# One layer of a hybrid streaming encoder on one core: GpSimd in order of emission, small copies moved to VectorE, rests and stores of the delta-rule jobs placed anew

## The chip, the cores and the metric

The program runs on one core of one Trainium2 chip. A core has a matrix engine (TensorE, in the profile PE for the products and PEld for loading their stationary operand), a vector engine (VectorE, DVE), a scalar engine (ScalarE, ACT), a general engine (GpSimd, POOL) and SyncE (SP), which in this program issues the transfers between HBM and the on-chip memories. Each engine works through a list of its own, in order, and stops at an instruction whose inputs or whose destination are not ready.

The metric is the device time of one execution, in microseconds. The kernel before takes 2979.81 us, the median of three runs from 2978.62 to 2980.59.

## The reference

One encoder layer takes 512 prompt frames and 64 sample frames of width 2048, all in float32. What it computes, shortened:

```
mod = silu(c) @ w_ada + b_ada                       # six vectors of shift, scale and gate
h   = rmsnorm(x, norm1) * (1 + sc1) + sh1
a_q, a_k, a_v, a_r, a_lr, b_q, b_k, b_v, b_g, b_beta, b_alpha = split(h @ w_in)
# group A: gated linear attention, 4 heads
o_a, s_gla = recurrence(gla_step, st_gla, a_q, a_k, a_v, log_a)
# group B: gated delta rule, 8 heads of 128
q, k, v = silu(causal_dwconv([b_q, b_k, b_v], st_conv, gdn_conv_w))    # width 4
q, k = l2norm(q) * 128**-0.5, l2norm(k)
# per block: S_t = a_t (I - b_t k_t k_t^T) S_{t-1} + b_t k_t v_t^T,  o_t = S_t^T q_t,
#   with a solve by the unit lower triangle (I + strict_lower(beta k k^T * decay))
o_b, s_gdn = recurrence(gdn_step, st_gdn, q, k, v, g, beta)
o   = rmsnorm_per_head([o_a, o_b]) * gain * silu(gates)
x   = x + g1 * (o @ w_out)
h   = rmsnorm(x, norm2) * (1 + sc2) + sh2
x   = x + g2 * conv_ffn(h)                         # w_up, causal conv of width 3, w_down
y   = rmsnorm(x, final_norm)
```

Beside y, the last states of both recurrences and the last columns ahead of both convolutions are outputs, for the prompt and for the sample.

## The kernel before

**Stages.** Up to about 205 us the program transposes x, works out the modulation and the first columns of the input projection. From 205 to 880 us it computes the input projection of the delta-rule group head by head, with the recurrences of the heads beside it; from 880 to 1280 us the other group and the output projection; from 1280 us on the feed-forward part. Weights are float32, split into a high part (ACT, L599) and the remainder (DVE, L600) from a raw tile that SP loads (L598), and each product is made of three.

**How other work is put beside the projections.** One column tile of the projection is 16 steps of 6 matmuls. After each step `tick` advances the jobs: Python generators, the first of which may do one step of its work. `yield` ends the step, `yield WAIT` lets the next job in the list have it, and `rest(n)` is n times WAIT, so n steps of the projection (about 6 matmuls each) pass before the job emits more. A second generator, `ada_block`, works out the vectors of modulation that are wanted later: it loads weights into `xr` (L764), sums products with a scalar on DVE (L770, L772), and adds over the partitions by matmuls with one column (L778).

**What sets the order.** The Tile framework takes the operations as emitted, finds the dependences, and orders each engine's list by priority and by its own model of costs. The operations of a job on DVE and ACT go through `_Sooner` (all have line L1623), which gives them a priority of 80 places ahead; GpSimd's don't. So the lists of two engines need not be in the order of emission.

**One head of the delta rule.** The tiles q, k, v and g of the projection pass the convolution `gdn_conv` (q, k, v): ACT and DVE empty the two halves of the PSUM tile into `cb`, four small GpSimd copies (L916 to L919) put the columns in front of each half and save the last three columns, and ACT and DVE sum four shifted products. `put_s` sends the sample's columns to HBM (L900). Then the job `gdn`:

- it loads the head's decays (L173), and ACT makes two exponential tiles of them, which GpSimd masks (L181, L182);
- it normalizes q and k: sums of squares, L137 on DVE (adds epsilon), L138 on GpSimd (power of -1/2);
- it forms the strict lower triangle a, and `inverse16` inverts its 16x16 diagonal blocks. The blocks go to HBM (L340) and come back with one block to a lane (four loads, L345). After `rest(REST_D)` GpSimd does the substitution, 30 instructions of which each needs the one ahead (L347 to L354); below this is "the chain". Its result goes to HBM (L355), comes back spread over the partitions (two loads, L358), and DVE expands it (two L362);
- three levels double the size of the inverses by matmuls (the first at L238), and the states are carried from block to block (matmuls L276 to L305, states on DVE);
- the head's output is normalized: squares and sums, L137, L138, a scaling on ACT, four transposes (L144), a product with the gate on DVE, and a store by SP.

`gdn_heads` emits the tiles q and k of head h+1 ahead of v and g of head h, so the job of head h+1 begins while that of head h is in its recurrence: the chain of head h+1 and the norm of head h lie close together.

**Names that recur.** `bank` is a PSUM tile of the pool that all jobs share; `m`, `qkv`, `s`, `st`, `sq` are tiles of SBUF; `wh`, `wl` and `raw` are parts and raw tiles of weights; `xr` and `acc` belong to `ada_block`; `cm` is what L358 loads.

```
REST_D, REST_X, REST_T, REST_N, REST_G = 8, 16, 2, 2, 3
```

Here REST_D stands between the lane loads and the chain, REST_X behind the expansion, REST_T behind the norm of q and k, REST_N ahead of the transposes of the output, and REST_G in the other group.

Of the kernel before, what the change touches and what calls it, by code (L numbers as in the profile page):

```python
# [8 lines left out]
F32 = mybir.dt.float32  # L9
# [3 lines left out]
ALU = mybir.AluOpType  # L13
# [3 lines left out]
P = 128  # L17
# [17 lines left out]
REST_D, REST_X, REST_T, REST_N, REST_G = 8, 16, 2, 2, 3  # L35
# [60 lines left out]
class Kern:  # L96
    def __init__(self, tc, ctx, i, o):
# [4 lines left out]
        self.c = {}  # L102
        self.jv, self.ja = _Sooner(tc, tc.nc.vector), _Sooner(tc, tc.nc.scalar)

# [23 lines left out]
    def small(self, w):  # L128
        return self.sp.tile([P, w], F32, tag=f"s{w}", name=self.name(f"s{w}"))
# [5 lines left out]
    def rsqrt(self, out, src, n, parts=P):  # L135

        self.nc.vector.tensor_scalar_add(out[:parts, :n], src[:parts, :n], EPS)  # L137
        self.nc.gpsimd.tensor_tensor(out[:parts, :n], out[:parts, :n], self.mhalf[:parts, :n], op=ALU.pow)  # L138
# [16 lines left out]
    def gdn(self, qF, kF, x, gain, hcols, gb_src, s0, s_out, o_put, last_level):  # L155
# [25 lines left out]
        nc.gpsimd.affine_select(du, du, pattern=[[0, 4], [1, P]], compare_op=ALU.is_ge, fill=0.0, base=0, channel_multiplier=-1)  # L181
        nc.gpsimd.affine_select(dl, dl, pattern=[[0, 4], [-1, P]], compare_op=ALU.is_gt, fill=0.0, base=0, channel_multiplier=1)  # L182
        if pair:
            nc.gpsimd.memset(du[0:64, :, 64:P], 0.0)
# [4 lines left out]
        junk = self.half()  # L189
# [122 lines left out]
        junk = self.half()  # L312
# [10 lines left out]
        V.tensor_tensor(kF, kF, x["gate"](), op=ALU.mult)  # L323
        o_put(kF)
# [6 lines left out]
    def inverse16(self, a):  # L331
# [4 lines left out]
        nc, c, G = self.nc, self.c, self.nc.gpsimd  # L336
        pitch = 4 * P
        d0 = self.dp.tile([8 * (16 * pitch + 16)], F32, tag="d0", bufs=2, name=self.name("d0"))
        d1 = self.dp.tile([2, 32, 256], F32, tag="d1", bufs=2, name=self.name("d1"))
        nc.sync.dma_start(d0[:P * pitch].rearrange("(p f) -> p f", p=P), a.rearrange("p b t -> p (b t)"))  # L340
        lane = self.m()[:32].rearrange("p (w f) -> p w f", w=2)
# [12 lines left out]
        G.tensor_copy(xt, xx.rearrange("p i j -> p j i"))  # L354
        nc.sync.dma_start(d1.rearrange("w q f -> q w f"), lane)  # L355
        cm = self.sp.tile([P, 2, 4, 16], F32, tag="cm", bufs=1, name=self.name("cm"))
        for w in range(2):
            nc.sync.dma_start(cm[:, w], d1[w].rearrange("(b n) (i j) -> (n i) b j", b=4, i=16))  # L358
        sh = [P, 4, 8, 16]
        t, u = self.m4(), self.m4()  # L360
# [3 lines left out]
        yield from self.rest(REST_X)  # L364
        return u, t

    def gla(self, nb, qF, kF, g, x, s0, s_out, o_put):
# [103 lines left out]
        for f in range(2):  # L471
# [4 lines left out]
            o_put(f, dst)  # L476
# [419 lines left out]
    def put_s(self, name, col, write):  # L896
# [3 lines left out]
        self.nc.sync.dma_start(self.sd[name][:, col * TS:(col + 1) * TS], t)  # L900
# [7 lines left out]
    def gdn_conv(self, ps, t, dst, name, h):  # L908
# [3 lines left out]
        cb = self.ap.tile([P, 582], F32, tag="cb", bufs=1, name=self.name("cb"))  # L912
# [772 lines left out]
```

## Time and profile before

| | us |
|---|---|
| median of three runs | 2979.81 (2978.62 to 2980.59) |
| the profiled execution, its own time | 2981.26 |
| span of the profiled execution | 2979.5 |
| PE busy | 2863.4 (96%), 21060 instructions |
| DVE busy | 2050.0 (69%), 3234 |
| ACT busy | 1179.3 (40%), 2015 |
| POOL busy | 338.0 (11%), 609 |
| mean granted clock of TensorE | 0.98 |

A line of a group gives the source line, the engine, the operation, its output and inputs with partitions by elements and the count; behind the bar stand the busy time and the mean in ns, and the idle time of the engine just before, with what ended it. A line of the timeline begins with start and duration in us, and a bracket at its end gives the wait just before it and what released it (a name after `<-`). A line with a stretch `A:B` gives the stretch's length and then each engine's busy time with its number of instructions, the granted clock of TensorE as a share of full speed, and the load of the transfers. SPq is SP's own list of transfers.

### The profile page before, as it was taken

How to read it: one execution, taken by the hardware profiler on the slowest of the kernel's cores; microseconds unless marked ns; L12 is line 12 of the kernel's file. 1: busy time of each engine (PE TensorE's matmuls, PEld its weight loads, DVE VectorE, ACT ScalarE, POOL GpSimd, SP SyncE). 2: the span in 40 equal slices, each digit the busy share in tenths (PEclk: the TensorE clock that was granted, in tenths of full speed). 3: DMA queues.
4: the chain of work that ended last, by engine and by line, in shares of the span. 5: the costliest groups of instructions: out<-in, count | busy, mean ns of one | idle time of the engine just before them, and what ended most of it. 6: DMA issues, size and time to landing. Idle time of an engine off the chain costs nothing.

```text
span 2979.5 us, 52341 instructions
## 1 busy us (share of the span) xinstructions
PE 2863.4 (96%) x21060; PEld 2772.9 (93%) x21060; DVE 2050.0 (69%) x3234; ACT 1179.3 (40%) x2015; POOL 338.0 (11%) x609
## 2 busy tenths in 40 slices
PE   6998899999899999999999999999999999999998
PEld 3688888999889998999999999999999999999997
DVE  2366766667668867557888888888888865555555
ACT  4234444444445333245444444444444421222223
POOL 0004323333120000000011111111111100000000
PEclk8999999999999999999999999999999999999999
DMA  8864544444454446643333333333333473333221
GB/s 269 285 185 121 150 143 124 128 129 144 134 159 130 137 132 194 199 140 97 106 105 111 109 103 107 111 102 105 115 105 105 133 236 101 111 101 113 84 85 66
DMA packets 535446, 395.55 MB, mean 133 GB/s; under 512 B 59657, under 2 KB 465412, under 8 KB 535204
## 3 DMA queue, kind: packets, MB, share of 16 engines
q1 hardware_dynamic: 535204, 392.21, 44.0%
q8 instruction: 166, 2.72, 0.4%
q14 instruction: 76, 0.62, 0.1%
HBM read 356.47 MB, written 35.67 MB: 132 GB/s over the span
## 4 chain that ended last, share of the span: by engine, by line
PE 71%; DVE 3%; DMA 2%; POOL 1%; issue 1%; ACT 1%; SPq 0%; ACTq 0%; DVEq 0%; POOLq 0%
PE g L512 22%; PE bank L1301 11%; PE bank L1300 11%; PE bank L1302 11%; PE g L514 11%; DVE acc L772 1%; PE bank L405 1%; PE bank L144 1%; DMA xr<-in_w_ada_dram 1%; DMA xr<-in_x_prompt_dram 1%; PE bank L778 1%; DVE wl L600 0%; POOL m L352 0%; POOL m L351 0%; POOL s L138 0%
## 5 line engine op out<-in xcount | busy, mean ns | idle before, releaser
L1301 PE MATMUL bank<-slot,wh 128*128 128x290 f32 x2464 | 736.3, 299 | 0.0
L1300 PE MATMUL bank<-slot,wh 128*128 128x290 f32 x2464 | 734.0, 298 | 0.0
L1302 PE MATMUL bank<-slot,wl 128*128 128x290 f32 x2464 | 728.2, 296 | 0.0
L512 PE MATMUL g<-slot,wh 128*128 128x288 f32 x3168 | 551.7, 295 | 0.3 <-DVE slot L1070 0.3
L512 PE MATMUL g<-hh,wh 128*128 128x288 f32 x2048 | 473.1, 310 | 0.0
L1302 PEld LDWEIGHTS bank<-slot,wl 128*128 128x128 f32 x2464 | 470.8, 191 | 0.0
L1301 PEld LDWEIGHTS bank<-slot,wh 128*128 128x128 f32 x2464 | 469.8, 191 | 0.1
L512 PEld LDWEIGHTS g<-slot,wh 128*128 128x128 f32 x3168 | 465.8, 188 | 0.7 <-DVE slot L1070 0.5
L599 ACT ACTIVATE wh<-raw 128x1024 fp32r<-128x1024 f32 x215 | 227.5, 1059 | 601.9 <-PE g L512 572.1
L1300 PEld LDWEIGHTS bank<-slot,wh 128*128 128x128 f32 x2464 | 464.2, 188 | 0.1
L512 PE MATMUL g<-hl,wh 128*128 128x288 f32 x2048 | 461.6, 304 | 0.0
L514 PE MATMUL g<-hh,wl 128*128 128x288 f32 x2048 | 459.9, 303 | 1.6 <-DVE wl L600 1.6
L1070 DVE SCALAR_TENSOR_TENSOR slot<-g,mod,slot 128x512 f32<-128x512 f32 (+1 forms) x448 | 202.1, 492 | 284.2 <-PE g L514 283.2
L772 DVE SCALAR_TENSOR_TENSOR acc<-xr,ct,acc 128x512 f32<-128x512 f32 x480 | 340.5, 752 | 26.6 <-DMA xr<-in_w_ada_dram 26.0
L512 PEld LDWEIGHTS g<-hh,wh 128*128 128x128 f32 x2048 | 336.6, 193 | 12.1 <-issue 9.8
L514 PEld LDWEIGHTS g<-hh,wl 128*128 128x128 f32 x2048 | 338.6, 193 | 8.4 <-issue 5.9
L512 PEld LDWEIGHTS g<-hl,wh 128*128 128x128 f32 x2048 | 340.4, 193 | 4.4 <-issue 3.9
L514 PE MATMUL g<-slot,wl 128*128 128x288 f32 x1584 | 342.8, 295 | 0.0
L600 DVE TENSOR_TENSOR wl<-raw,wh 128x1024 fp32r<-128x1024 f32 x215 | 262.5, 1221 | 62.4 <-ACT wh L599 61.7
L1247 ACT ACTIVATE wh<-raw 128x1024 fp32r<-128x1024 f32 x176 | 186.0, 1057 | 221.9 <-PE bank L1301 185.6
L514 PEld LDWEIGHTS g<-slot,wl 128*128 128x128 f32 x1584 | 255.3, 188 | 0.0
L1248 DVE TENSOR_TENSOR wl<-raw,wh 128x1024 fp32r<-128x1024 f32 x176 | 215.4, 1224 | 54.3 <-ACT wh L1247 54.3
(354 smaller groups left out, 3160.9 us busy)
## 6 DMA issues: line engine op xcount, KB each, us to landing
raw<-in_w_up_dram SPq DMA_DIRECT2D x176, 512.0 KB
xr<-in_w_ada_dram SPq DMA_DIRECT2D x128, 512.0 KB
raw<-in_w_in_dram SPq DMA_DIRECT2D x100, 512.0 KB
raw<-in_w_down_dram SPq DMA_DIRECT2D x88, 512.0 KB
hraw<-in_w_ada_dram SPq DMA_DIRECT2D x64, 512.0 KB
raw<-in_w_out_dram SPq DMA_DIRECT2D x32, 512.0 KB
slot<-actd SPq DMA_DIRECT2D x44, 288.0 KB
actd<-v SPq DMA_DIRECT2D x44, 256.0 KB
```

The source lines that it names most:

```text
L144: self.nc.tensor.transpose(ps[:, b * P:(b + 1) * P], src4[:, b], self.c["ident"])
L512: T.matmul(ps[:, h if bank is None else bank, :n], wh, x[:, h, :n], start=f, stop=False)
L514: T.matmul(ps[:, h if bank is None else bank, :n], wl, ah[:, h, :n], start=False, stop=stop)
L599: nc.scalar.activation(hi[:, :n_], raw[:, :n_], AF.Copy)
L600: nc.vector.tensor_tensor(lo[:, :n_], raw[:, :n_], hi[:, :n_].bitcast(F32), op=ALU.subtract)
L772: V.scalar_tensor_tensor(acc[s], w[:, k], col, acc[s], op0=ALU.mult, op1=ALU.add)
L1070: self.nc.vector.scalar_tensor_tensor(x1[:, :, z], ps[:, :, c], gain[:, q:q + 1], x1[:, :, z], op0=ALU.mult, op1=ALU.add)
L1247: self.nc.scalar.activation(hi, src, AF.Copy)
L1248: self.nc.vector.tensor_tensor(lo, src, hi.bitcast(F32), op=ALU.subtract)
L1300: T.matmul(ps, wh[:, j], hi, start=(c < 3 and j == 0), stop=False, skip_group_check=True)
L1301: T.matmul(ps, wh[:, j], lo, start=False, stop=False, skip_group_check=True)
L1302: T.matmul(ps, wl[:, j], hi, start=False, stop=(j == NPAIR - 1), skip_group_check=True)
```

## The change

- GpSimd's operations of the mixers go through a new class `_InTurn`, which tells the scheduler to issue each behind the one emitted last. They so keep the order of emission.
- The rests are placed anew. In `inverse16` there are now rests ahead of the store of the blocks (2), between that store and the lane loads (3), between the lane loads and the chain (6 instead of 8), ahead of the store of the chain's result (2), between it and its loads (3), ahead of DVE's expansion (4) and behind it (4 instead of 16). Ahead of the transposes of the output there are 4 instead of 2, and 4 ahead of the output's store, in both groups.
- In `gdn_conv`, `cb` becomes one tile that lives through all heads; its zero columns are written once, by DVE, ahead of the first head. The columns of the old state are copied by DVE, and the last columns of both halves by one DVE copy instead of two on GpSimd. The 96 copies of GpSimd (4 in each of 24 convolutions) are gone; DVE has 49 more.
- `put_s` issues its transfer from ACT instead of SP, but for one name ("ag"): 43 transfers.
- The small tiles of sums (`small`) come from 8 buffers; what squares and sums write beside their sums goes to one lasting scrap tile instead of a tile of `half`.

PE's instructions are the same in both kernels. The diff, cut to its core:

```diff
-REST_D, REST_X, REST_T, REST_N, REST_G = 8, 16, 2, 2, 3
+REST_S, REST_L, REST_D, REST_X, REST_U, REST_T, REST_N, REST_O, REST_G = 2, 3, 6, 4, 4, 2, 4, 4, 3
...
+        self.pool = _InTurn(tc, tc.nc.gpsimd)
...
     def small(self, w):
-        return self.sp.tile([P, w], F32, tag=f"s{w}", name=self.name(f"s{w}"))
+        return self.sp.tile([P, w], F32, tag=f"s{w}", bufs=8, name=self.name(f"s{w}"))
...
-        self.nc.gpsimd.tensor_tensor(out[:parts, :n], out[:parts, :n], self.mhalf[:parts, :n], op=ALU.pow)
+        self.pool.tensor_tensor(out[:parts, :n], out[:parts, :n], self.mhalf[:parts, :n], op=ALU.pow)
...
-        junk = self.half()
+        junk = self.junk()
...
         V.tensor_tensor(kF, kF, x["gate"](), op=ALU.mult)
+        yield from self.rest(REST_O)
         o_put(kF)
...
-        nc, c, G = self.nc, self.c, self.nc.gpsimd
+        nc, c, G = self.nc, self.c, self.pool
...
+        yield from self.rest(REST_S)
         nc.sync.dma_start(d0[:P * pitch].rearrange("(p f) -> p f", p=P), a.rearrange("p b t -> p (b t)"))
+        yield from self.rest(REST_L)
...
         G.tensor_copy(xt, xx.rearrange("p i j -> p j i"))
+        yield from self.rest(REST_S)
         nc.sync.dma_start(d1.rearrange("w q f -> q w f"), lane)
+        yield from self.rest(REST_L)
...
         sh = [P, 4, 8, 16]
+        yield from self.rest(REST_X)
         t, u = self.m4(), self.m4()
...
-        yield from self.rest(REST_X)
+        yield from self.rest(REST_U)
...
-        self.nc.sync.dma_start(self.sd[name][:, col * TS:(col + 1) * TS], t)
+        (self.nc.sync if name == "ag" else self.nc.scalar).dma_start(self.sd[name][:, col * TS:(col + 1) * TS], t)
...
-        cb = self.ap.tile([P, 582], F32, tag="cb", bufs=1, name=self.name("cb"))
+        cb = self.conv_in
...
-        nc.gpsimd.tensor_copy(cb[:, 0:3], self.zero3)
-        nc.gpsimd.tensor_copy(cb[:, 515:518], self.vmap["st_conv"].rearrange("p (i t) -> p t i", i=3)[:, t])
-        nc.gpsimd.tensor_copy(self.cs[:, 0, :, t], cb[:, 512:515])
-        nc.gpsimd.tensor_copy(self.cs[:, 1, :, t], cb[:, 579:582])
+        V.tensor_copy(cb[:, 515:518], self.vmap["st_conv"].rearrange("p (i t) -> p t i", i=3)[:, t])
...
+        V.tensor_copy(self.cs[:, :, :, t], cb[:, 512:646].rearrange("p (s c) -> p s c", s=2)[:, :, 0:3])
...
+class _InTurn:
+    def __init__(self, tc, engine):
+        self.tc, self.engine, self.last = tc, engine, None
+    def __getattr__(self, name):
+        f = getattr(self.engine, name)
+        def g(*a, **kw):
+            with self.tc.issue_after(self.last) if self.last is not None else nullcontext():
+                r = f(*a, **kw)
+            self.last = self.tc.nc.cur_bb.bb.instructions[-1]
+            return r
+        return g
```

What this does to the lists of the engines is seen at three places. In the rows below, names with their running numbers differ from one kernel to the other, and the lines are those of the kernel that the row is from.

GpSimd, around the norm of the first head: `s_425` (before) and `s_418` (after) is its root, the `m_2516` and `m_2556` with 32 partitions are lanes of the second head's chain. Before:

```order
L352 TENSOR_TENSOR m_2516<-m_2516 32x2x13
L351 TENSOR_TENSOR m_2516<-m_2516 32x14
L352 TENSOR_TENSOR m_2516<-m_2516 32x14
L354 COPY m_2516<-m_2516 32x256
L138 TENSOR_TENSOR s_425_2868<-s_425_2868,mhalf 128x4
L918 COPY cs<-cb_3049 128x3
L919 COPY cs<-cb_3049 128x3
L916 COPY cb_3192<-zero_100 128x3
L917 COPY cb_3192<-cols 128x3
```

And now, where every operation of GpSimd has the line of the class's helper:

```order
L1657 COPY m_2154<-m_2154 32x256
L1657 AFFINE_SELECT m_2396<-m_2396 128x512
L1657 AFFINE_SELECT m_2395<-m_2395 128x512
L1657 TENSOR_TENSOR kt_2411<-kt_2411,mhalf 128x4
L1657 TENSOR_TENSOR rq_2443<-rq_2443,mhalf 128x4
L1657 TENSOR_TENSOR s_418_2854<-s_418_2854,mhalf 128x4
L1657 MEMSET m_2556 32x16
L1657 TENSOR_TENSOR m_2556<-m_2556 32x14 x2
L1657 TENSOR_TENSOR m_2556<-m_2556 32x13x2 x2
```

The root of the first head stood behind the whole chain of the second; it now stands ahead of it. The same holds for the later heads.

VectorE, around the norm of the third head: L137 is its addition of epsilon (L145 now), L362 the expansion for the fourth head (L376 now), L600 the remainder of a split (L616 now). Before:

```order
L1623 SCALAR_TENSOR_TENSOR st_4433<-st_4389,egl,bank_4431 128x128
L1623 SCALAR_TENSOR_TENSOR sq_4446<-bank_4445,kt_3363,m_4326 128x128
L1623 SCALAR_TENSOR_TENSOR st_4468<-st_4433,egl,bank_4466 128x128
L362 TENSOR_TENSOR m_4726<-cm_4723,consts_1740 128x512
L600 TENSOR_TENSOR wl_4711<-raw_4709,wh_4710 128x1024
L362 TENSOR_TENSOR m_4727<-cm_4723,consts_1740 128x512
L137 TENSOR_SCALAR s_655_4483<-s_654_4482 128x4
L1623 TENSOR_TENSOR qkv_3191<-qkv_3191,gt_4524 128x512
```

And now:

```order
L1642 SCALAR_TENSOR_TENSOR sq_4405<-bank_4404,kt_3342,m_4285 128x128
L1642 SCALAR_TENSOR_TENSOR st_4427<-st_4392,egl,bank_4425 128x128
L616 TENSOR_TENSOR wl_4665<-raw_4663,wh_4664 128x1024
L145 TENSOR_SCALAR s_637_4442<-s_636_4441 128x4
L1642 TENSOR_TENSOR qkv_3173<-qkv_3173,gt_4481 128x512
L616 TENSOR_TENSOR wl_4734<-raw_4732,wh_4733 128x1024
L376 TENSOR_TENSOR m_4776<-cm_4744,consts_1740 128x512
L376 TENSOR_TENSOR m_4777<-cm_4744,consts_1740 128x512
L786 TENSOR_SCALAR acc_4643<-xr_4645,ct 128x512
```

The expansion stood ahead of the third head's addition and its gate; it now stands behind both, with a split between.

SyncE, around the store of the first head's chain (L355, now L367) and the load of the second head's decays (L173, now L181). Before:

```order
L598 DMA raw_2887<-in_w_in_dram 128x8x128
L764 DMA xr_2635<-in_w_ada_dram 128x2x512
L355 DMA d_318_2117<-m_2119 32x2x256
L900 DMA sd_k<-ts_2394 128x64
L598 DMA raw_2971<-in_w_in_dram 128x8x128
L358 DMA cm_2343<-d_318_2117 128x4x16 x2
L598 DMA raw_3066<-in_w_in_dram 128x8x128
L173 DMA m_2410<-gd 128x512
L598 DMA raw_3136<-in_w_in_dram 128x8x128
```

And now:

```order
L350 DMA d_314_2112<-m_2083 128x512
L614 DMA raw_2751<-in_w_in_dram 128x8x128
L356 DMA m_2154<-d_314_2112 8x16x16 x4
L181 DMA m_2393<-gd 128x512
L780 DMA xr_2624<-in_w_ada_dram 128x2x512
L614 DMA raw_2872<-in_w_in_dram 128x8x128
L614 DMA raw_2950<-in_w_in_dram 128x8x128
L614 DMA raw_3042<-in_w_in_dram 128x8x128
L367 DMA d_315_2113<-m_2154 32x2x256
L371 DMA cm_2469<-d_315_2113 128x4x16 x2
```

The load of the decays stood behind the store of the chain's result; it now stands ahead of it, as do three more loads of weights, and the store of the sample's columns (L900) is no longer in this list.

More of the change, by code (lines that the diff above doesn't have):

```diff
@@ L101, in __init__ @@
         self.pg = ctx.enter_context(tc.tile_pool(name="pg", bufs=2, space=PSUM))
-        self.c = {}
+        self.c, self.scrap = {}, []
         self.jv, self.ja = _Sooner(tc, tc.nc.vector), _Sooner(tc, tc.nc.scalar)
+        self.pool = _InTurn(tc, tc.nc.gpsimd)
     def load_consts(self, pool, names):
@@ L128, in small, with junk @@
     def small(self, w):
-        return self.sp.tile([P, w], F32, tag=f"s{w}", name=self.name(f"s{w}"))
+        return self.sp.tile([P, w], F32, tag=f"s{w}", bufs=8, name=self.name(f"s{w}"))
+    def junk(self):
+        if not self.scrap:
+            self.scrap.append(self.kp.tile([P, P], F32, name="scrap"))
+        return self.scrap[0]
     def half(self):
@@ L180, in gdn @@
         A.activation(du, du, AF.Exp, scale=-1.0)
-        nc.gpsimd.affine_select(du, du, pattern=[[0, 4], [1, P]], compare_op=ALU.is_ge, fill=0.0, base=0, channel_multiplier=-1)
-        nc.gpsimd.affine_select(dl, dl, pattern=[[0, 4], [-1, P]], compare_op=ALU.is_gt, fill=0.0, base=0, channel_multiplier=1)
+        self.pool.affine_select(du, du, pattern=[[0, 4], [1, P]], compare_op=ALU.is_ge, fill=0.0, base=0, channel_multiplier=-1)
+        self.pool.affine_select(dl, dl, pattern=[[0, 4], [-1, P]], compare_op=ALU.is_gt, fill=0.0, base=0, channel_multiplier=1)
         if pair:
-            nc.gpsimd.memset(du[0:64, :, 64:P], 0.0)
+            self.pool.memset(du[0:64, :, 64:P], 0.0)
         A.activation(gb, gb, AF.Exp)
         ss, kt = self.small(8), self.sp.tile([P, 4, 4], F32, tag="kt", bufs=3, name=self.name("kt"))
-        junk = self.half()
+        junk = self.junk()
         kps = self.transpose4(kF)
@@ L311, in gdn @@
         ss, rr = self.small(8), self.small(8)
-        junk = self.half()
+        junk = self.junk()
         for b in range(4):
@@ L475, in gla @@
             V.tensor_tensor(dst, dst, x[f"gate{f}"](), op=ALU.mult)
-            o_put(f, dst)
+        yield from self.rest(REST_O)
+        for f in range(2):
+            o_put(f, (qd, kd3)[f])
     def tick(self):
@@ L966, in vg @@
             x["gate"] = lambda: b4(gt)
+        self.conv_in = self.ap.tile([P, 646], F32, name="conv_in")
+        nc.vector.tensor_copy(self.conv_in[:, 0:3], self.zero3)
         xs = [qk(0)]
```

## The prediction

> **What bounds the kernel now.** I read the page first, then the busy time by stage, then what TensorE (PE) waited for in the stage that the change touches, and then the queues behind each of those waits.
>
> ```profile
> span 2979.5 us, 52341 instructions
> core 0: us, PE busy (x) PEld busy (x) DVE busy (x) ACT busy (x) POOL busy (x), PEclk, DMA share, GB/s
> 205.00:880.00 675.00, 618.86 (x4549) 599.01 (x4548) 442.44 (x765) 310.29 (x771) 202.03 (x405) 0.95 0.48 138
> 1280.00:2980.00 1700.00, 1684.07 (x12578) 1680.85 (x12576) 1231.16 (x1743) 655.81 (x852) 116.66 (x157) 1.00 0.36 110
> ```
>
> PE sets the end everywhere. From 1280 us on it is busy 99% at a granted clock of 1.00, with 1684.07/12578 = 0.134 us for a matmul; nothing there is touched. The mixers of the delta rule stand at 205 to 880 us: PE is idle for 56 us there, and its clock is 0.95. PE's instructions are the same in both programs, so the change can only act through these idle gaps and the clock behind them. Seven gaps make up three quarters of the idle time:
>
> ```profile
> 271.57 0.77 PE L778 MATMUL bank<-consts,acc 128*128 128x1 f32 x3 [8.26 <-DVE m L1623]
> 313.60 0.47 PE L144 MATMUL bank<-consts,m 128*128 128x128 f32 x1 [9.14 <-ACT m L1623]
> 382.24 0.47 PE L144 MATMUL bank<-consts,m 128*128 128x128 f32 x1 [4.64 <-ACT m L1623]
> 460.30 0.47 PE L144 MATMUL bank<-consts,m 128*128 128x128 f32 x1 [4.90 <-ACT m L1623]
> 536.36 0.47 PE L144 MATMUL bank<-consts,m 128*128 128x128 f32 x1 [4.07 <-ACT m L1623]
> 609.86 0.47 PE L144 MATMUL bank<-consts,m 128*128 128x128 f32 x1 [2.36 <-ACT m L1623]
> 760.83 0.58 PE L276 MATMUL bank<-st,qkv 128*128 128x128 f32 x1 [8.75 <-DVE st L1623]
> ```
>
> The bracket is the gap and what ended it: 42.1 us in all. The five at L144 are the transposes of a head's normed output. Behind each gap PE runs slow for a while (the column PEclk):
>
> ```profile
> 271.60:278.70 7.10, 7.10 (x32) 7.10 (x33) 2.71 (x11) 4.24 (x15) 1.01 (x1) 0.50 0.00 0
> 313.60:319.60 6.00, 6.00 (x26) 5.99 (x27) 3.79 (x7) 3.57 (x7) 1.15 (x2) 0.50 0.59 179
> 382.20:388.00 5.80, 5.76 (x25) 5.75 (x26) 1.64 (x3) 1.55 (x4) 0.00 (x0) 0.51 0.93 248
> 460.30:466.40 6.10, 6.10 (x26) 6.08 (x27) 0.69 (x1) 2.09 (x6) 0.00 (x0) 0.50 0.40 124
> 536.40:541.50 5.10, 5.10 (x22) 5.07 (x23) 0.69 (x1) 4.13 (x13) 0.00 (x0) 0.50 0.35 104
> 609.90:613.30 3.40, 3.40 (x15) 3.38 (x16) 2.04 (x4) 3.17 (x8) 0.00 (x0) 0.52 0.55 163
> 760.90:766.80 5.90, 5.90 (x26) 5.85 (x26) 4.32 (x9) 2.14 (x10) 0.11 (x1) 0.50 0.73 214
> ```
>
> These are 39.4 us at half clock, so half of that, 19.7 us, is lost. The seven gaps cost 42.1 + 19.7 = 61.8 us. The Trainium skill, TensorE: Matmul & The Clock Gate, Part 1, puts the half rate behind an idle window of about 3.4 us; by that the 2.36 us gap would cost its own length alone, and the sum would be 1.7 us smaller. The row at 609.90 shows 0.52 behind that very gap, so the trace decides.
>
> **Who is late.** The first head's norm (gap at 313.60):
>
> ```profile
> 301.43 0.39 PE L305 MATMUL bank<-st,qkv 128*128 128x128 f32 x2
> 305.31 0.33 SPq L355 DMA_DIRECT2D d<-m  x1
> 309.62 0.75 DVE L772 SCALAR_TENSOR_TENSOR acc<-xr,ct,acc 128x512 f32<-128x512 f32 x1 [7.86 <-DMA xr<-in_w_ada_dram]
> 311.43 0.16 DVE L137 TENSOR_SCALAR s<-s 128x4 f32<-128x4 f32 x1
> 311.67 1.44 POOL L138 TENSOR_TENSOR s<-s,mhalf 128x4 f32<-128x4 f32 x1 [6.39 <-DVE s L137]
> ```
>
> The head's last product is done at 301.8. Its root needs L137 on VectorE (DVE), then L138 on GpSimd (POOL), but DVE stands at L772, whose weights are issued by SP behind L355. L355 stores what POOL's substitution for the next head's 16x16 inverses (L347 to L354, "the chain") yields, and holds SP until 305.31. The 8.75 us gap has the same cause: DVE waits for the same load.
>
> ```profile
> 757.97 1.42 DVE L772 SCALAR_TENSOR_TENSOR acc<-xr,ct,acc 128x512 f32<-128x512 f32 x2 [9.14 <-DMA xr<-in_w_ada_dram]
> 376.67 0.27 DVE L137 TENSOR_SCALAR s<-s 128x4 f32<-128x4 f32 x1
> 380.75 1.01 POOL L138 TENSOR_TENSOR s<-s,mhalf 128x4 f32<-128x4 f32 x1
> 456.21 0.69 DVE L362 TENSOR_TENSOR m<-cm,consts 128x512 f32<-128x512 f32 x1 [4.46 <-DMA cm<-d]
> 458.56 0.16 DVE L137 TENSOR_SCALAR s<-s 128x4 f32<-128x4 f32 x1
> ```
>
> At 376.67 (second head) DVE is in time, and POOL takes the root 4 us later, since the whole chain stands ahead of it. At 456.21 (third head) it is DVE's order: L362, which expands the inverses, stands ahead of L137 and waits for the chain's blocks to come back. The gaps at 536.36 and 609.86 have that order too. The first gap is ACT's, which waits for the decays (L173), a load that SP issues behind the first chain's L355:
>
> ```profile
> 259.95 1.19 SPq L173 DMA_DIRECT2D m<-gd  x1
> 264.60 0.98 ACT L1623 ACTIVATE m<-m,ncum 128x128 f32<-128x128 f32 x3 [8.20 <-DMA m<-gd]
> ```
>
> So one thing, the next head's chain started ahead of this head's norm, blocks SP, DVE or POOL in turn.
>
> **The change part by part.** *GpSimd in order of emission, with the rests placed anew.* The order shown ahead has POOL's root ahead of the chain in every head, DVE's L137 ahead of L362, and the first L173 ahead of L355. What then stood behind the chain stands ahead of it, so all seven causes go. What is left of each I work out by its shortest path. For the norm: L305 ends at 301.8, and the squares, L137 (0.2 us) and L138 (1.44 us) take about 2.8 us, when nothing is in the way. PE has 12 to 30 matmuls of cover there, 1.6 to 4.0 us at 0.134. That leaves 0 to 1.3 us of gap; I take 1 us for each of six norms, 6 us, too short to lower the clock (0 to 12). At the first gap PE now comes to L778 three matmuls behind the transposes and waits for ACT to empty a bank; an estimate of 2.5 us and 1.7 us of clock, 4.2 (0 to the 11.8 that it costs now).
>
> *The price: the chain now starts only behind the root.* How long it then takes depends on DVE:
>
> ```profile
> 289.40:305.30 15.90, 15.02 (x111) 13.84 (x110) 11.26 (x20) 6.05 (x21) 13.70 (x31) 1.00 0.39 105
> 442.10:452.70 10.60, 10.55 (x73) 9.06 (x72) 3.09 (x9) 4.11 (x15) 8.38 (x31) 1.00 0.33 99
> 736.10:753.40 17.30, 15.95 (x119) 14.98 (x117) 12.50 (x20) 6.58 (x17) 15.20 (x33) 1.00 0.29 91
> 331.72 0.44 PE L238 MATMUL bank<-m,m 128*128 128x64 f32 x3
> 764.93 0.42 PE L305 MATMUL bank<-st,qkv 128*128 128x128 f32 x1
> 792.22 0.44 PE L238 MATMUL bank<-m,m 128*128 128x64 f32 x3
> ```
>
> The three stretches are chains from first to last instruction: 15.9 and 17.3 us while DVE is busy 70%, 10.6 while it is busy 29%. From the end of a chain to L362 it is 456.21 - 452.70 = 3.5 us, and the two L362 take 1.3. So the inverses are ready 2.8 + (10.6 to 17.3) + 3.5 + 1.3 = 18.2 to 24.9 us behind L305. PE wants them at L238. From the seventh head's last product (764.93) to the eighth head's L238 that is 26.9 us, 26.2 without the clock's loss: enough, by 1.3 us at the least. For the second head it is 331.72 - 301.8 = 29.9 us, but 9.14 and 3.0 of that go away with its gap; with 11 matmuls more between the two in the new order 19.3 us are left. DVE is busy there, so 2.8 + 15.9 + 3.5 + 1.3 = 23.5: 4.2 us late, with 1.7 us of clock 5.9. I put 2 us more on each of two later heads, since loads now stand between SP's L355 and L358 for heads 6 to 8: 9.9 us in all (0 to 33, below).
>
> A rule of the Trainium skill speaks against this part: GPSIMD Engine Reference, Key points, says that POOL shares its interfaces to SBUF with VectorE and contends with instructions that have two SBUF inputs, as L772 has. The stretches above agree (17.3 against 10.6 us). If by this rule every chain took 17.3 us, the second head would be 5.6 us late instead of 4.2, and the sum 2 to 4 us worse.
>
> *Conv ends by VectorE.* 96 POOL copies go:
>
> ```profile
> L916 POOL COPY cb<-zero 128x3 f32<-128x3 f32 x22 | 21.4, 974 | 83.4 <-DVE ca L922 79.1 <-ACT wh L599 4.3
> 264.37 0.22 DVE L915 COPY cb<-g 128x64 f32<-128x64 f32 x1
> 741.60 0.34 SPq L900 DMA_DIRECT2D sd_v<-ts  x1
> ```
>
> POOL loses copies of about a microsecond each, with long waits that held up what followed; that gain is in the sum already. DVE takes 49 copies of at most 0.22 us (a larger copy's time): 11 us on an engine that is idle for a third of this stage. Two stand within a conv's own path, which PE sees at a few transposes: 2 us (0 to 5).
>
> *Stores of the sample's columns issued by ACT instead of SP.* 43 issues at 0.34 us leave SP. ACT's price is not in the trace; between 0 and twice SP's it is 0 to 29 us, beside 365 us in which ACT is idle in this stage. I take SP's 0.34, off PE's path, 0 us; if that cover were gone, 15.
>
> *More tiles for the sums, one scratch tile, later output stores (REST_O), four more table loads on ACT.* They take waits away or lie in the same idle time; 0.
>
> The sum: 61.8 - 6 - 4.2 - 9.9 - 2 = 39.7 us. The profiled execution took 2981.26 us for its span of 2979.5; the median of the runs is 1.5 us less, 2979.81, so the prediction is 2979.8 - 39.7 = 2940 us.
>
> **The rivals.** *The chain becomes the new wait at every head.* For it speaks that the chain begins some 13 us later against the head's products, and the second head is short by my own sum; against it the 26.2 us at the eighth head. With 3 us and 1.7 of clock at seven heads it costs 33 us in place of 9.9: 2979.8 - (61.8 - 6 - 4.2 - 33 - 2) = 2963 us.
>
> *DVE parked at L362 starves PE: slower.* In the new order the fourth head's L362 stands right behind L137, and splits of weights, the emptying of PE's banks and the next block's L770 are queued behind it. Were the inverses 8 us later than PE's need at seven heads, each gap would cost 8 and 3 of clock, 77 us against the 61.8 - 12.2 = 49.6 that remain: 2979.8 + 27 = 3007 us. It decides from 7 us a head on. Against it: the 24.9 us at worst stay under the 26.2, and while DVE is parked the chain takes 10.6 us.
>
> *The gaps only move.* If DVE or SP remains late for another reason (the loads behind the later L355), the same gaps end at another line: 2979 us. Against it: the seven causes above all name the chain, and the order moves each.
>
> **How the numbers follow.** The forecast has a chance of 0.75, the chain as new wait 0.13, the slower case 0.08, no change 0.04. Two times of this kernel differ by about 0.2% (6 us) without meaning anything. Faster by more: the first two cases and no other, less a little for their tails, 0.87; the same 0.05; slower 0.08. Downwards, nothing left behind gives 2979.8 - 61.8 = 2918, and the smaller gaps that I have not counted (about 14 us of the 56) could give a few more: 2912. Upwards the range takes in the first rival and a little beyond, 2968.
>
> **What would show it.** In the new profile PE's clock in the mixers rises from 0.95 to 0.97 or more, and the waits of L144 for ACT's scaling by the root fall to about 1 us each. POOL's root runs within 3 us of the head's last product, and the chain behind it. The wait of PE for the inverses' first product at the second head should be 2 to 7 us and absent at heads 3 to 6. DVE's longest wait is still L362, now harmless. I am wrong if PE waits at L238 at each head, if weights' splits end PE's gaps, or if L144's gaps stay above 3 us.

## The result, and the profile after

The changed kernel is slower. Its median is 3002.81 us (3001.61 to 3013.53, four runs), that of the kernel before, beside it, 2980.20 us (2978.62 to 2984.36). The ratio is 1.0082, with a 95% interval from 1.0056 to 1.0107. On another chip it was 1.0075 (1.0063 to 1.0088; e12 in the table below).

The profiled execution is the slowest of the four, 3013.53 us with a span of 3011.7 us. Some 5.6 us of that stand ahead of the first product of the projections (which begins at 70.3 us, before at 64.8), where the clock was at half rate for longer; TensorE's work there is the same, and the profile of the run on the other chip has a span of 3005.9 us. The rest of the difference grows from 560 us on. Up to there the changed kernel has even done a little more (3466 instructions of TensorE against 3436); from 560 to 880 us it does 2056 against 2234. Some 10 us more are lost between 880 and 1280 us, an estimate from 17.5 us of idle time there instead of 9.9 and from 17.0 us at half clock instead of 10.2. The longest new wait there, 4.4 us at L419 of the other group, is in e2 below too, which loses nothing as a whole; this part was not taken apart further.

The waits of TensorE (PE) from 205 to 900 us, and those of VectorE (DVE), in the changed kernel (microseconds in all, times, the longest). L152 are now the transposes, L246 and L252 the two products of a level of the inverse (L238 and L244 before), L376 the expansion (L362 before), L788 a product of the modulation (L772 before), and L1642 and L1657 the helpers of the jobs on VectorE and ScalarE, and on GpSimd:

```profile
PE bank L252 <- DVE conv_in L932: 14.2, 3, 5.2
PE bank L252 <- DVE m L1642: 14.2, 3, 6.6
PE bank L246 <- DVE m L376: 12.5, 5, 4.1
PE bank L152 <- ACT m L1642: 6.7, 8, 1.5
PE bank L246 <- DVE sq L998: 3.4, 1, 3.4
```

```profile
DVE m L376 <- DMA cm<-d: 45.6, 5, 11.1
DVE acc L788 <- DMA xr<-in_w_ada_dram: 35.6, 9, 12.9
```

The stage from 205 to 880 us, with its busy times and TensorE's clock, which was 0.95 before:

```profile
205.00:880.00 675.00, 615.45 (x4448) 593.52 (x4447) 439.91 (x803) 309.70 (x766) 150.73 (x309) 0.94 0.47 135
```

So the gaps that the prediction meant to remove are gone: the transposes wait 6.7 us for the scaling by the root, in eight places, and the long waits at L778 and L276 have no successor. In their place stand waits at the levels of the inverse, 44.3 us in these rows. Most are of 3 to 7 us, and the clock falls behind them, so that PE does 4448 instructions in this stage instead of 4549. The clock is the larger part of that: PE's idle time in the stage grows by 3.4 us only (from 56.1 to 59.6), but from 205 to 900 us, read in windows of 0.1 us, the granted clock is at half rate for 89.4 us instead of 68.2, which costs half of the 21 us between them.

How such a gap comes about is seen at the third head, in the order of time:

```profile
374.37 1.44 POOL L1657 TENSOR_TENSOR s<-s,mhalf 128x4 f32<-128x4 f32 x1 [24.25 <-DVE s L145]
375.83 10.86 POOL L1657 TENSOR_TENSOR m<-m 32x14 f32<-32x14 f32 x28
390.92 1.29 DVE L376 TENSOR_TENSOR m<-cm,consts 128x512 f32<-128x512 f32 x2 [8.33 <-DMA cm<-d]
390.56 0.58 SPq L181 DMA_DIRECT2D m<-gd  x1
395.29 1.28 ACT L1642 ACTIVATE m<-m,ncum 128x128 f32<-128x128 f32 x4 [7.08 <-DMA m<-gd]
397.27 2.54 DVE L936 SCALAR_TENSOR_TENSOR ca<-conv_in,cols,ca 128x579 f32<-128x579 f32 x3 [3.59 <-ACT ca L934]
404.57 4.16 DVE L788 SCALAR_TENSOR_TENSOR acc<-xr,ct,acc 128x512 f32<-128x512 f32 x5
408.65 0.41 DVE L1642 TENSOR_TENSOR m<-bank,consts 128x256 f32<-128x256 f32 x1
409.21 1.94 PE L252 MATMUL bank<-m,m 128*128 128x64 f32 x8 [5.15 <-DVE conv_in L932]
```

The root is on time. The chain starts behind it, at 375.8, and VectorE reaches L376 8.3 us before the chain's result is back. While it stands there, its other work piles up. Then it waits 3.6 us more, for ScalarE, which waits 7.1 us for the next head's decays (L181): SP issues that load behind the chain's store and loads. VectorE works off its products of the modulation when TensorE has already done L246 (at 402.1), and the copy that L252 needs (408.65) stands behind five of them. The wait is named after conv_in, the instruction behind the copy in VectorE's list; what TensorE needs is the copy.

### The profile page after: what moved, and what is told of

Same layout as the page of the kernel before. It is cut to its first block, busy times and chain, and to the rows that moved or that the text cites. A ratio compares the mean times of both kernels' runs of the same rounds, so it can differ in the third digit from the quotient of the medians.

```text
span 3011.7 us, 52193 instructions
## 1 busy us (share of the span) xinstructions
PE 2885.0 (96%) x21060; PEld 2788.5 (93%) x21060; DVE 2055.7 (68%) x3283; ACT 1185.1 (39%) x2019; POOL 286.6 (10%) x513
## 4 chain that ended last, share of the span: by engine, by line
PE 74%; issue 9%; DVE 6%; POOL 5%; DMA 4%; ACT 2%; SPq 1%; ACTq 0%; POOLq 0%; DVEq 0%
PE g L528 23%; PE bank L1320 11%; PE g L530 11%; PE bank L1319 11%; PE bank L1321 11%; POOL m L1657 4%; DVE acc L788 2%; PE bank L688 1%; DMA xr<-in_w_ada_dram 1%; PE bank L152 1%; PE bank L419 1%; DMA m<-gd 1%; ACT m L1642 1%; PE bank L252 1%; DMA xr<-in_x_prompt_dram 1%
## 5 line engine op out<-in xcount | busy, mean ns | idle before, releaser
L788 DVE SCALAR_TENSOR_TENSOR acc<-xr,ct,acc 128x512 f32<-128x512 f32 x480 | 341.7, 752 | 44.0 <-DMA xr<-in_w_ada_dram 43.5
L528 PEld LDWEIGHTS g<-hh,wh 128*128 128x128 f32 x2048 | 337.0, 193 | 17.5 <-issue 10.0
L616 DVE TENSOR_TENSOR wl<-raw,wh 128x1024 fp32r<-128x1024 f32 x215 | 262.0, 1218 | 51.8 <-ACT wh L615 51.2
```

The lines of the kernel that those rows point to most:

```text
L528: T.matmul(ps[:, h if bank is None else bank, :n], wh, x[:, h, :n], start=f, stop=False)
L616: nc.vector.tensor_tensor(lo[:, :n_], raw[:, :n_], hi[:, :n_].bitcast(F32), op=ALU.subtract)
L788: V.scalar_tensor_tensor(acc[s], w[:, k], col, acc[s], op0=ALU.mult, op1=ALU.add)
```

## The experiments

All ratios are to the kernel before on the same chip. "Levels" are PE's waits at the two products of a level of the inverse, "transposes" those at the transposes for any cause, "stands" the waits of VectorE at the expansion and at the products of the modulation for loads; all are sums of rows of the views of waits from 205 to 900 us, in one profiled execution each.

| kernel | ratio (95%) | levels | transposes | VectorE stands: expansion + loads |
|---|---|---|---|---|
| before | 1 | 3.7 | 33.1 | 46.5 + 21.2 |
| changed | 1.0082 (1.0056 to 1.0107) | 44.6 | 10.6 | 45.6 + 35.6 |
| e1: chain's store and loads by GpSimd | 1.0068 (1.0053 to 1.0083) | 52.1 | 10.7 | 75.5 + 5.2 |
| e2: changed, without `_InTurn` | 0.9992 (0.9980 to 1.0003) | 11.4 | 43.0 | 12.1 + 20.7 |
| e3: changed, rests of before | 1.0093 (1.0078 to 1.0108) | 48.8 | 12.8 | 85.7 + 11.3 |
| e4: before, with `_InTurn` alone | 1.0094 (1.0079 to 1.0109) | 51.3 | 11.0 | 83.9 + 18.0 |
| e5: changed, expansion later in VectorE's list | 0.9991 (0.9981 to 1.0002) | 34.0 | 9.9 | 20.6 + 38.5 |
| e6: changed, modulation in turn with the jobs | 1.0151 (1.0132 to 1.0170) | 30.5 | 19.6 | 10.7 + 54.8 |
| e7: e6, and the expansion in turn too | 1.0150 (1.0133 to 1.0167) | 35.4 | 20.1 | 10.2 + 55.1 |
| e8: changed, chain on VectorE | 0.9831 (0.9809 to 0.9854) | 0.6 | 15.5 | 10.6 + 6.5 |
| e9: before, chain on VectorE | 0.9835 (0.9821 to 0.9848) | 0.9 | 16.5 | 10.0 + 6.2 |
| e10: changed, convolution's copies on GpSimd | 1.0083 (1.0070 to 1.0097) | 46.4 | 10.4 | 49.3 + 36.5 |
| e11: changed, sample's stores by SP | 1.0079 (1.0066 to 1.0093) | 45.3 | 13.3 | 48.7 + 35.1 |
| e12: changed, as it is | 1.0075 (1.0063 to 1.0088) | 46.9 | 10.5 | 46.5 + 38.0 |
| e13: e1 and e5 together | 0.9999 (0.9987 to 1.0012) | 33.3 | 9.5 | 40.0 + 7.3 |

### Which part of the change costs the time

The four first runs ask for the part and for the road. At the sixth head of the changed kernel SP seemed to be the road: its store L367 waits for the chain, and the loads behind it leave VectorE without weights for 12 us.

```profile
612.43 14.34 POOL L1657 TENSOR_TENSOR m<-m 32x14 f32<-32x14 f32 x28
627.49 0.31 SPq L367 DMA_DIRECT2D d<-m  x1
628.98 1.18 SPq L780 DMA_DIRECT2D xr<-in_w_ada_dram  x2
634.31 4.73 DVE L788 SCALAR_TENSOR_TENSOR acc<-xr,ct,acc 128x512 f32<-128x512 f32 x7 [12.38 <-DMA xr<-in_w_ada_dram]
```

e1, the chain's store and loads issued by GpSimd:

```diff
-        nc.sync.dma_start(d1.rearrange("w q f -> q w f"), lane)
+        nc.gpsimd.dma_start(d1.rearrange("w q f -> q w f"), lane)
...
-            nc.sync.dma_start(cm[:, w], d1[w].rearrange("(b n) (i j) -> (n i) b j", b=4, i=16))
+            nc.gpsimd.dma_start(cm[:, w], d1[w].rearrange("(b n) (i j) -> (n i) b j", b=4, i=16))
```

> The changed kernel, but the store of the chain's result (L367) and its two loads (L371) are issued by GpSimd, behind the chain, instead of SP. GpSimd's order, TensorE's order and the rests stay. Theory SP (the later chain holds SP at L367, the weights queued behind it land late, VectorE parks at L788 for xr and then comes late to L376 and to the copies between L246 and L252): the parking of VectorE at L788 for xr falls from 35.6 us to under 15, TensorE's waits at L246 and L252 fall from 47 us in all to under 25, and the time falls to 2970 to 2987 us. Rival CHAIN (the inverses are late because the chain starts only behind the root, whoever issues the store): the waits at L246 and L252 stay within 10 us of 47, 2995 to 3005 us.

e2, no `_InTurn`:

```diff
-        self.pool = _InTurn(tc, tc.nc.gpsimd)
+        self.pool = tc.nc.gpsimd
```

> The changed kernel without the class _InTurn: GpSimd's order is left to the scheduler, which again puts the chain of the next head ahead of the root of this head at five of eight heads and, at two, the root into the middle of the chain. Theory CHAIN: the chains start up to 10 us earlier, L246 and L252 lose more than half of their 47 us, L152 for ACT's scaling gets 10 to 25 us back; 2975 to 2990 us. Theory SP: SP is held about as long, but earlier, so part of the loss goes: 2985 to 2995 us. If the rests are the cause, nothing changes: 2998 to 3006 us.

e3, the rests of before:

```diff
-REST_S, REST_L, REST_D, REST_X, REST_U, REST_T, REST_N, REST_O, REST_G = 2, 3, 6, 4, 4, 2, 4, 4, 3
+REST_S, REST_L, REST_D, REST_X, REST_U, REST_T, REST_N, REST_O, REST_G = 0, 0, 8, 0, 16, 2, 2, 0, 3
```

> The changed kernel with the rests of the kernel before (0, 0, 8, 0 ahead of the expansion, 16 behind it, 2, 2, 0), all else as changed. GpSimd still has the root ahead of the chain. Theory RESTS (the store and the gather of the blocks are emitted 5 steps later and the expansion has 4 steps instead of 16 to be done, so VectorE has 8 products of the modulation where it had 22 between L376 and the first copy, but no time to be late): the waits at L246 and L252 fall below 20 us and the time to 2960 to 2980 us. Theories SP and CHAIN: the chain still starts behind the root, SP still waits for it; 2990 to 3005 us.

e4, the kernel before with the class `_InTurn`, and the same operations as in the change sent through it:

```diff
+        self.pool = _InTurn(tc, tc.nc.gpsimd)
...
-        self.nc.gpsimd.tensor_tensor(out[:parts, :n], out[:parts, :n], self.mhalf[:parts, :n], op=ALU.pow)
+        self.pool.tensor_tensor(out[:parts, :n], out[:parts, :n], self.mhalf[:parts, :n], op=ALU.pow)
...
-        nc, c, G = self.nc, self.c, self.nc.gpsimd
+        nc, c, G = self.nc, self.c, self.pool
```

> The kernel before, with the class _InTurn alone added: the root stands ahead of the next chain at every head. What the prediction costed: the five gaps at L144 fall from 25 us to under 8, and if the chain has room, 2945 to 2960 us. Theories SP and CHAIN: the gaps at L144 fall, but gaps at L238 and L244 come in their place, 2975 to 2995 us. Theory RESTS: 2945 to 2970 us.

The part is `_InTurn`. Alone, it makes the kernel before slower by 0.94% (e4); without it, the rest of the change is worth nothing that can be told (e2, 0.9992); and with the rests of before the loss is 0.93% (e3) beside 0.75% (e12), on two chips and with intervals that overlap. So the rests are not the cause.

Not every expectation held. e1 (3006.86 us), e3 (3013.55) and e4 (3014.08) lie above the longest times that were expected of them, 3005, 3005 and 2995 us. The chip explains some of it, since the kernel before takes 8.5 us more there (2988.69), but not e4: no theory had allowed for so much. And e2 gave the transposes 32 us back, where 10 to 25 were expected.

The waits change place with the class. With the class alone (lines of that kernel: L145 the transposes, L239 and L245 the levels):

```profile
PE bank L245 <- DVE cb L916: 29.9, 4, 9.6
PE bank L245 <- DVE m L1624: 9.0, 1, 9.0
PE bank L239 <- DVE m L363: 7.8, 1, 7.8
PE bank L145 <- ACT m L1624: 6.4, 8, 1.2
```

And without it, in e2:

```profile
PE bank L152 <- ACT m L1642: 39.0, 8, 9.4
PE bank L252 <- DVE cs L939: 6.2, 1, 6.2
```

The road over SP falls with e1. With SP freed, VectorE no longer stands for the modulation's weights, and so it reaches L376 sooner and stands there:

```profile
DVE m L376 <- DMA cm<-d: 75.5, 9, 11.7
```

Its standing is 80.7 us in all, as in the changed kernel (81.2), and the time is the same. The theory on SP had taken the place where VectorE stands for the cause of its standing.

### By which road it reaches TensorE

e5 moves the expansion in VectorE's list behind the last product of the modulation that was emitted ahead of it:

```diff
+                    self.last_ada = nc.cur_bb.bb.instructions[-1]      # in ada_block, behind each L786 and L788
...
-            nc.vector.tensor_tensor(x.rearrange(...), ...)
+            with self.tc.issue_after(self.last_ada):
+                nc.vector.tensor_tensor(x.rearrange(...), ...)
```

> The changed kernel, but VectorE's two L376 are issued behind the last product of the modulation (L788) emitted ahead of them, so they come later in VectorE's list; GpSimd still has the root ahead of the chain. Theory PARK (the chain that now starts behind the root finds VectorE already standing at L376; while it stands, its other work piles up, and the copies between L246 and L252 come late): the parking at L376 falls from 45.6 us to under 20, the waits of TensorE at L246 and L252 from 47 us to under 25, and the ratio to the kernel before from 1.008 to 0.993 to 1.000. Rival LATENCY (root, chain, transfers and expansion are too long for the room, wherever VectorE stands): the waits at L246 and L252 stay within 10 us of 47, ratio 1.005 to 1.010.

e6 puts each product of the modulation behind the last operation of the jobs instead, and e7 the expansion too; in both, GpSimd stays in order of emission:

```diff
+                    with self.tc.issue_after(self.jv.last):
                         V.scalar_tensor_tensor(acc[s], w[:, k], col, acc[s], op0=ALU.mult, op1=ALU.add)
...
+            with self.tc.issue_after(self.jv.last):                    # e7 alone
                 nc.vector.tensor_tensor(x.rearrange(...), ...)
```

> The changed kernel, but each product of the modulation on VectorE (L786, L788) is issued behind the last operation of the head jobs on VectorE emitted ahead of it, so that such products no longer stand ahead of a copy between L246 and L252 (3 or fewer where there were up to 13). Theory PARK: the copies come on time even after VectorE has stood at L376; waits at L252 fall from 31 us to under 12, those at L246 stay near 16; ratio 0.990 to 0.999. Rival LATENCY: the waits at L252 stay over 20 us, or move to L246; ratio 1.003 to 1.010.

> The same kernel as the one with the modulation's products in turn, and VectorE's L376 too behind the last operation of the head jobs emitted ahead of it; GpSimd in order of emission as in the changed kernel. Theory PARK: as good or better than with the products in turn alone, ratio 0.985 to 0.998. Rival LATENCY: 1.003 to 1.010.

e8 takes the chain off GpSimd altogether:

```diff
-        nc, c, G = self.nc, self.c, self.pool
+        nc, c, G = self.nc, self.c, self.jv
```

> The changed kernel, but the chain's 30 instructions a head run on VectorE instead of GpSimd, so root and chain share no engine. They add 270 small instructions to VectorE, at 0.2 us each 54 us to its 442 in this stage. Theory PARK and rival LATENCY alike: roots are on time and the chain need not wait for them; where the chain is ready 8 us or more ahead of L246, the waits at L246, L252 and L152 fall together from 54 us to under 30, ratio 0.990 to 1.000. If VectorE's load is what makes everything late (rival LOAD), the ratio is 1.008 to 1.025.

e5 brought back what `_InTurn` costs (0.9991), with GpSimd's list unchanged. Its waits (L377 and L1644 are L376 and L1642 there):

```profile
PE bank L246 <- DVE m L377: 15.0, 5, 4.1
PE bank L252 <- DVE m L1644: 14.5, 5, 5.1
DVE acc L789 <- DMA xr<-in_w_ada_dram: 38.5, 12, 12.3
DVE m L377 <- DMA cm<-d: 20.6, 3, 9.8
```

Head by head: at the third and the fourth, where VectorE had stood 8.3 and 7.6 us at the expansion, it now does not stand there, and the gaps at L252 (5.2 and 4.6 us) are gone. At the fifth to seventh the edit moved the second of the two expansions by one place of the list or none, and the gaps at L246 and L252 are still there (3 to 5 us each). So at two heads the expansion's place in VectorE's list, and with it the standing, is shown to be what makes the level late; the waits that remain, 34 us, missed the 25 expected.

e6 and e7 missed both expectations. The wait at L252 did shrink, but VectorE, held to the order of emission, now stood at the modulation's products themselves (54.8 us for loads), and TensorE waited in turn for the sums of the modulation:

```profile
PE bank L795 <- DVE acc L789: 13.6, 2, 7.5
```

```profile
205.00:880.00 675.00, 608.97 (x4401) 588.90 (x4400) 436.71 (x784) 304.24 (x761) 161.86 (x296) 0.93 0.47 131
```

So a level's copy that comes sooner in the list was paid for with standing at loads (54.8 against 35.6 us) and a clock of 0.93. Why e6 loses further behind 880 us was not followed up.

e13 closes both places at which VectorE stands, with the edits of e1 and e5 together:

> Both edits together: the chain's store and loads issued by GpSimd (L367, L371), and VectorE's L376 behind the last product of the modulation emitted ahead of it. Alone, the first left the ratio at 1.007 (VectorE, free of the loads behind SP, stood at L376 for 75 us instead of 46) and the second brought it to 0.999 (VectorE still stood 38 us for loads behind SP). Theory PARK, in its full form (VectorE is late because it stands, at whichever of the two places): with both its standing at L376 and L788 together falls below 35 us, the waits at L246 and L252 from 34 us to under 15, ratio 0.985 to 0.994. Rival LATENCY (root, chain, transfers and expansion need the whole room): the waits stay at 25 us or more, ratio 0.997 to 1.003.

The ratio is 0.9999, and the numbers are those of the rival LATENCY: the waits at the levels stay at 33 us. But VectorE's standing fell to 47 us only, not below 35, since the expansion was again not moved at the fifth to seventh heads. The sixth head (L377, L1659 and L1644 are L376, L1657 and L1642 here):

```profile
595.30 1.44 POOL L1659 TENSOR_TENSOR s<-s,mhalf 128x4 f32<-128x4 f32 x1 [22.19 <-DVE s L145]
596.77 18.07 POOL L1659 TENSOR_TENSOR m<-m 32x14 f32<-32x14 f32 x28
622.18 0.69 DVE L377 TENSOR_TENSOR m<-cm,consts 128x512 f32<-128x512 f32 x1 [8.20 <-DMA cm<-d]
624.26 1.10 PE L246 MATMUL bank<-m,m 128*128 128x64 f32 x8 [0.23 <-DVE m L377]
633.39 1.94 PE L252 MATMUL bank<-m,m 128*128 128x64 f32 x8 [7.17 <-DVE cs L941]
```

Here the inverses are ready just as TensorE comes for them (a gap of 0.23 us), behind a chain of 18 us: root, chain, transfers and expansion use the whole room. And VectorE, which stood 8.2 us for them, has the next copy 7.2 us late. Both roads are in these rows. It is the same at the fifth and the seventh: VectorE stands 3.6 and 7.0 us at the expansion, L246 then waits 0 and 0.6 us, and L252 4.9 and 6.6. So at these three heads nearly all the waiting is at L252, where VectorE's backlog puts it, though the sum is what LATENCY had said. How much of it would be left if VectorE did not stand was not separated, and stays open.

### Root and chain on different engines

In e8 the two no longer compete: the root need not wait for the chain, nor the chain for the root. The expectation was 0.990 to 1.000; measured was 0.9831. e9 asks whether anything of the change is needed for that. Its one edit to the kernel before:

```diff
-        nc, c, G = self.nc, self.c, self.nc.gpsimd
+        nc, c, G = self.nc, self.c, self.jv
```

> The kernel before with one edit: the chain's 30 instructions a head run on VectorE (with the priority of the head jobs), not on GpSimd. None of the change is in it. If root and chain sharing GpSimd is the whole matter, the gaps at L144 and the waits for L355 go as they did with the changed kernel's chain on VectorE (ratio 0.983): ratio 0.978 to 0.988. If the changed kernel's other parts (rests, small copies on VectorE, stores issued by ScalarE) are needed for that gain, VectorE's order keeps L362 ahead of L137 and some gaps stay: ratio 0.988 to 0.997.

It is not. e9 has 0.9835 (0.9821 to 0.9848), 2935.62 us beside 2985.66 us on its chip: faster than both kernels by 50 us or more, and as fast as e8. In e9 the stage, VectorE's wait at the expansion, and one shape of the chain's instructions (L1623 is the helper of the jobs there):

```profile
205.00:880.00 675.00, 649.12 (x4912) 625.31 (x4912) 523.61 (x1121) 334.74 (x825) 113.44 (x136) 0.99 0.53 148
```

```profile
DVE m L362 <- DMA cm<-d: 10.0, 6, 4.4
```

```profile
L1623 DVE TENSOR_TENSOR m<-m 32x56 f32<-32x56 f32 x36 | 7.2, 201 | 0.8
```

The same shape on GpSimd, in the kernel before:

```profile
L352 POOL TENSOR_TENSOR m<-m 32x56 f32<-32x56 f32 x18 | 6.9, 385 | 1.4
L351 POOL TENSOR_TENSOR m<-m 32x56 f32<-32x56 f32 x18 | 6.5, 363 | 1.4
```

VectorE, busy 442 us of the stage's 675 before, takes some 80 us more in it (with more of the program done by its end) and stands 16 us instead of 68. The clock is 0.99. An instruction of this shape takes 201 ns there, 363 to 385 on GpSimd. The Trainium skill, GPSIMD Engine Reference, Key points, puts VectorE at about twice GpSimd's speed for elementwise work; these rows, 1.8 to 1.9, agree.

That the instructions are shorter is hardly what gains, though, for VectorE does other work between them, and the chains as a whole are not shorter. The first and the last of the second head's chain in e9:

```profile
293.09 0.07 DVE L1623 MEMSET m<- 32x16 f32 x1
320.51 0.37 DVE L1623 COPY m<-m 32x256 f32<-32x256 f32 x1
```

That is 27.8 us, where the kernel before took 15.9 on GpSimd; over the nine chains it is 7.6 to 32.3 us in e9, 17.2 in the mean, and 10.1 to 17.3 in the kernel before, 13.4 in the mean. PE waits only 0.9 us at the levels all the same. The edit also gives the chain the jobs' priority on VectorE (`self.jv`); its part was not separated.

### The other parts

e10 restores the convolutions' tile and their four GpSimd copies, e11 SP as the issuer of the sample's columns, and e12 is the changed kernel unchanged, on the same chip.

```diff
-        V.tensor_copy(cb[:, 515:518], self.vmap["st_conv"].rearrange("p (i t) -> p t i", i=3)[:, t])
+        nc.gpsimd.tensor_copy(cb[:, 0:3], self.zero3)
+        nc.gpsimd.tensor_copy(cb[:, 515:518], self.vmap["st_conv"].rearrange("p (i t) -> p t i", i=3)[:, t])
+        nc.gpsimd.tensor_copy(self.cs[:, 0, :, t], cb[:, 512:515])
+        nc.gpsimd.tensor_copy(self.cs[:, 1, :, t], cb[:, 579:582])
```

```diff
-        (self.nc.sync if name == "ag" else self.nc.scalar).dma_start(self.sd[name][:, col * TS:(col + 1) * TS], t)
+        self.nc.sync.dma_start(self.sd[name][:, col * TS:(col + 1) * TS], t)
```

> The changed kernel with the convolutions as in the kernel before: a cb tile for each, and four small copies of each convolution on GpSimd again, which are not kept in turn, so they stand between the chain's instructions. Theory PARK: the copies lengthen the chains and so the time that VectorE stands at L376, by 1 to 3 us a head: 0.2 to 0.6% slower than the changed kernel on the same chip. What the prediction costed (2 us of loss from the move to VectorE): within 0.2% of the changed kernel.

> The changed kernel, but the stores of the sample's columns are all issued by SP again, as before. What the prediction costed at 0 us (up to 15 us of gain now if ScalarE's issues lay on the path): within 0.2% of the changed kernel. If SP's time behind the chain is short, the stores queued there make the weights later: 0.2 to 0.5% slower.

> The changed kernel as it is, for the comparison on one chip: ratio to the kernel before 1.006 to 1.010.

1.0083, 1.0079 and 1.0075, with intervals that overlap: neither part can be told from nothing. The premise of e10's first theory was wrong, too: in GpSimd's list the copies stand behind the chains, and only two of them inside one, the first head's.

## Why the prediction was wrong, point by point

**What bounds the kernel, and who is late: right.** The seven gaps were there, and GpSimd's order of root and chain was behind them. e9 bears it out in the other direction: with the two on different engines the kernel gains 50 us, against the 61.8 us that the gaps were said to cost.

**What is left of the seven gaps: right.** 6 us were put on six norms; the transposes wait 6.7 us for the scaling in eight places. The first gap, put at 4.2 us, is gone, and so is that at L276. But the clock of the stage, which was to rise from 0.95 to 0.97 or more, is 0.94.

**The price of the chain behind the root: the step that failed.** 9.9 us stood for it, of which 4.2 us were gap at the second head, and nothing at heads 3 to 6. The first of these held:

```profile
323.41 0.90 PE L246 MATMUL bank<-m,m 128*128 128x64 f32 x3 [4.12 <-DVE m L376]
```

But the gaps of L246 and L252 come to 44.6 us in the changed kernel, where the kernel before has 3.7, and the clock, which was to give back 19.7 us, loses instead (89.4 us at half rate, before 68.2). The step compared "18.2 to 24.9 us behind L305" with the 26.2 us until PE wants the inverses, and found "enough, by 1.3 us at the least". Two things were left out of it, and a third was not what failed:

- The sum ends at the first product. The second needs a copy by VectorE, and VectorE has a backlog after it stood. At the third and fourth head the first product was on time and the second 5.2 and 4.6 us late.
- The sum lets L362 run as soon as its load has landed. At the sixth head the blocks were requested by 631.4 us and the expansion began at 642.4, because VectorE had stood 12.4 us for loads that SP held behind L367, and then had other work ahead of it. "So all seven causes go" was wrong for this one: other loads now stand behind the store of the chain's result, and e1 shows that with SP free VectorE stands at L376 instead.
- The lengths of the chain held. In the changed kernel the nine chains take 11.0 to 16.5 us from first to last instruction, against the 10.6 to 17.3 of the sum; they are short, 11.5 us, at the third and fourth head, where VectorE stands. In e13 two took longer, 18.8 and 19.6 us at the sixth and seventh head. The Trainium skill, GPSIMD Engine Reference, Key points, has the two engines share their interfaces to SBUF; these lengths agree, though no run here tested that by itself.

**The rivals.** "DVE parked at L362 starves PE", with a chance of 0.08, comes nearest to what happened. Its mechanism, the work queued behind the parked instruction, is shown at the third and fourth head (e5), and open as the cause at the others. Its point of decision, 7 us a head, was near: the waits at L246 and L252 were 3 to 8 us together at each of the second to the eighth head and the sample's. Its time, 3007 us, is near the measured 3002.81 partly by luck: it put TensorE's waits at late inverses, where most are at the second product of a level. Against it stood that the inverses are ready in time even "at worst" and that the chain is short while VectorE stands, as if standing cost nothing. "The chain becomes the new wait at every head" had the place, but with 3 us a head it was sized too small, and so left a gain (2963 us). "The gaps only move" is the best short account of the profile: 33.1 us of waits at the transposes became 10.6, 3.7 at the levels became 44.6.

**The parts costed at 2 us or nothing: right.** Copies, stores, tiles and rests together change the time by less than can be told (e2), and so do copies and stores one by one (e10 and e11 beside e12). The tiles had no run of their own.

**The forecast of 2940 us** is near what e8 and e9 reach (their ratios of 0.983 make 2930 us of 2980), by removing the competition; the change mostly reversed who waits.

## What to carry to other kernels

When two jobs compete for one in-order engine, putting one ahead moves the wait to the other's consumers; look first whether one of them fits on another engine, as a chain of tiny instructions did here between VectorE's other work, though it was no shorter as a whole. A latency budget must run to the last product that needs the result, through every copy between, and must charge a parked in-order engine for the work that piles up behind it. And where freeing one queue leaves the time as it was, compare the sum of an engine's waits over all places, not the wait that went away.

## What the runs showed of the hardware that was not expected

TensorE's clock fell to half without a gap of a fifth of a microsecond. In the changed kernel 16 products with a single column (the sums of the modulation over the partitions) run at 685.88 us, TensorE counts as busy throughout, and the next 3.4 us are granted at half rate:

```profile
685.88 1.84 PE L794 MATMUL bank<-consts,acc 128*128 128x1 f32 x16
684.00:687.70 3.70, 3.70 (x31) 3.29 (x30) 0.71 (x3) 1.05 (x4) 0.00 (x0) 0.99 0.52 132
687.70:691.10 3.40, 3.40 (x16) 3.40 (x16) 1.81 (x5) 0.28 (x1) 0.00 (x0) 0.50 0.00 0
```

A single gap of 1.65 us at 440.5, beside transposes, was followed by another such 3.4 us from 441.9 on. The Trainium skill, TensorE: Matmul & The Clock Gate, Part 1, names an idle window of about 3.4 us as the condition. The stretches at half rate do have lengths of 3.4 us and its multiples (from 205 to 900 us, 3.4 to 10.3 us before and 3.4 to 17.1 in the changed kernel), but in this trace less than a window of idle time was enough.
